# The first block of the down products in another order of groups, with seven pairs of tiles in seven products instead of five

## The chip, the cores and the metric

The kernel runs on one core of a Trainium2 chip. The metric is the time of one execution on the device, in microseconds (us). Five engines of the core work side by side, each through its own instructions in order: TensorE (PE in the profile), VectorE (DVE), ScalarE (ACT), GpSimd (POOL) and SyncE (SP), whose queue issues the transfers from memory.

## The reference

One decoder layer on 256 tokens of width 2048, in float32: a half feed-forward, retention and sliding-window attention side by side, a second half feed-forward, and a gated per-layer embedding. The change touches the feed-forward, which occurs twice (f1 and f2):

```python
D_MODEL, SEQ, D_FF = 2048, 256, 5632

def swiglu(x, w_gu, w_down):
    g, u = jnp.split(x @ w_gu, 2, axis=-1)
    return (jax.nn.silu(g) * u) @ w_down

h = layer_norm(alpha * h + 0.5 * swiglu(h, w_ffn1_gu[i], w_ffn1_down[i]), ln_g[i, 0], ln_b[i, 0])
...   # mixers
h = layer_norm(alpha * h + 0.5 * swiglu(h, w_ffn2_gu[i], w_ffn2_down[i]), ln_g[i, 2], ln_b[i, 2])
```

The down product `@ w_down` sums over 5632 = 44 tiles of 128 activations and gives 2048 columns.

## The kernel before, in words

**Numbers in two parts.** Every operand of a product is split into a high and a low part (`split`, L100 and L101): ScalarE casts the value to the high part (hi), VectorE subtracts to get the low part (lo). A product is three matmuls (`Sum.add`, L376 to L378): low by high, high by high, high by low. Each matmul here has 512 columns.

**Pairs and their two ways.** A pair p is two of the 44 tiles (p runs from 0 to 21). A block of the down product makes all 256 tokens of 1024 columns, which are two halves of tokens by two column blocks of 512. For one pair that is a 2 by 2 by 2 product of tiles. Done plainly ("P") it takes eight products, 24 matmuls; its weights are two chunks of 128x1024 (`Single`), for each of them one cast and one subtraction. Done in sevens ("S", class `Seven`) it takes seven products, 21 matmuls: the weights' two raw chunks are first combined by four VectorE additions of 128x512 (L172 to L175), then split in four pieces (VectorE instructions: `lf` 128x1024, `bf` 128x512, `luf` and `lvf` 128x1024), eight VectorE instructions in all, with four casts on ScalarE. The seven products of one S are in the order p1, q2, q3, q5, p7, p6, q4; the last S of a block has them in the order p1, q5, p6, p7, q2, q3, q4. After the last S of a block `fold` adds the sums that the sevens share (`seven_common`) to the residual.

**Activations.** The gu stage leaves the activations in 11 groups of four tiles, group g holding the pairs 2g and 2g+1. `convert(g)` splits a group in high and low part (f1ah, f1al). A group that is used in sevens needs `seven_forms` too: four VectorE additions of 128x256 (L447 to L450), a cast on ScalarE and a subtraction on VectorE (f1forms). `SEVEN_DOWN = (6, 7, 8, 9)` names the groups that have these sums; the second block (d1, columns 1024 to 2047) uses all eight of their pairs as S, in turn with P, and isn't touched by the change.

**Order.** Each engine's order is the program's. `down_units` lists the units of the first block (d0) and of the second (d1); `block` walks the list, calls `before_unit(u)` ahead of unit u, and takes each unit's weights from a queue. The queue is planned in the same order: after a unit is used, `fill` makes the next ones (cast, subtract, and the additions of an S) while the units that stand ready have less than 45 matmuls, and issues loads as long as slots are free. So VectorE gets its work for weights some 36 to 45 matmuls ahead of TensorE, in program order, and the work for activations is put between by `before_unit(u)`: it converts one group ahead of each even u, four units before the group is used, and makes the forms. VectorE's instructions do not wait for that point of the program on TensorE, only for their data and for a free slot. In f1 the rotary table (`rotary_table`, L820 to L850) is woven in during the first units of d0 as well.

**The first block before.** P0 to P11 (groups 0 to 5), then S12 P13 S14 P15 S16 P20 S17 P21 S18 P19: five S. The forms of groups 6 to 9 are made ahead of units 2, 4, 6 and 8, while the plain pairs run.

Of the kernel before, what the change touches and what calls it, by code (L numbers as in the profile page):

```python
# [15 lines left out]
P = 128  # L16
S = 256
# [9 lines left out]
KF = FF // P  # L27
# [18 lines left out]
AHEAD_SLOTS = 32  # L46

SEVEN_DOWN = (6, 7, 8, 9)

BIG = 3.0e38  # L50
MAGIC = 12582912.0
# [6 lines left out]
def layer(ctx: ExitStack, tc: tile.TileContext, io):  # L58
# [16 lines left out]
    def slot(shape, dt, name):  # L75
        return slots.tile(shape, dt, tag="slot", name=name)
# [22 lines left out]
    def split(dst_hi, dst_lo, src, lo_engine=None):  # L99
        act.copy(dst_hi, src)  # L100
        (lo_engine or dve).tensor_tensor(dst_lo, src, dst_hi, ALU.subtract)  # L101
# [200 lines left out]
    def slots_for_weights(n, ahead=45, far=90):  # L302
        room.update(slots=n, ahead=ahead, far=far)
# [136 lines left out]
    def seven_forms(full, hi, lo):  # L440


        a11, a21 = (full[:, 0::2, t * P : (t + 1) * P] for t in range(2))
        a12, a22 = (full[:, 1::2, t * P : (t + 1) * P] for t in range(2))
        raw = slot([P, 8, P], F32, "sums")
        f5, f6, f7, f3 = (raw[:, 2 * j : 2 * j + 2, :] for j in range(4))
        dve.tensor_tensor(f5, a21, a22, ALU.subtract)  # L447
        dve.tensor_tensor(f7, a11, a21, ALU.subtract)
        dve.tensor_tensor(f6, f5, a11, ALU.subtract)
        dve.tensor_tensor(f3, a12, f6, ALU.add)  # L450
        split(hi, lo, raw)
        return lambda e: [(hi[:, 2 * j + e, :], lo[:, 2 * j + e, :]) for j in range(4)]
# [295 lines left out]
    def load_columns(src, col, name):  # L748
        v = slot([P, 2, 512], F32, f"{name}{col}")
        sync.dma_start(v, src[col])  # L750
        return v
# [64 lines left out]
    def rotary_table(nm):  # L816

        inv, sgn = (0, 2) if nm == "r" else (1, 3)
        pos_i = slot([P, S], I32, "pos_i" + nm)
        act.dma_start(pos_i, io["positions"].broadcast_to([P, S]))  # L820
        pos = slot([P, S], F32, "pos" + nm)
        yield
        dve.tensor_copy(pos, pos_i)
        table = slot([P, 2, S], F32, "trig" + nm)
        cos, sin = trig[nm] = table[:, 0, :], table[:, 1, :]
        w = slot([P, 4, S], F32, "rot" + nm)
        ang, n, na, nb = (w[:, j, :] for j in range(4))
        dve.tensor_scalar(ang, pos, cst[:, inv : inv + 1], None, ALU.mult)
        dve.tensor_scalar(n, ang, INV_2PI, MAGIC, ALU.mult, ALU.add)
        dve.tensor_scalar(n, n, MAGIC, None, ALU.subtract)  # L830
        dve.tensor_scalar(na, n, 1.0 / 2048.0, MAGIC, ALU.mult, ALU.add)
        dve.tensor_scalar(na, na, MAGIC, 2048.0, ALU.subtract, ALU.mult)
        dve.tensor_tensor(nb, n, na, ALU.subtract)
        yield
        for who, j in ((na, 0), (nb, 0), (na, 1), (nb, 1), (na, 2), (nb, 2), (na, 3)):
            dve.scalar_tensor_tensor(ang, who, -TWO_PI[j], ang, ALU.mult, ALU.add)
            if who is nb:
                yield
        yield
        dve.tensor_scalar(n, ang, 3.1415925, -3.1415925, ALU.min, ALU.max)  # L840
        yield
        act.activation(nb, n, AF.Sin)
        yield
        dve.tensor_scalar(sin, nb, cst[:, sgn : sgn + 1], None, ALU.mult)
        dve.tensor_scalar(na, ang, 1.5707963267948966, None, ALU.add)
        dve.tensor_scalar(n, na, 3.141592653589793, -6.283185307179586, ALU.is_gt, ALU.mult)
        dve.tensor_tensor(na, na, n, ALU.add)
        dve.tensor_scalar(na, na, 3.1415925, -3.1415925, ALU.min, ALU.max)
        yield
        act.activation(cos, na, AF.Sin)  # L850
        yield
# [13 lines left out]
    def down_units(n_held):  # L865


        first = [("P", p) for p in range(2 * SEVEN_DOWN[0])]
        g = SEVEN_DOWN[0]
        sevens = [2 * h for h in SEVEN_DOWN[:3]] + [2 * SEVEN_DOWN[2] + 1, 2 * SEVEN_DOWN[3]]  # L870
        plain = [p for p in range(2 * g, KF // 2) if p not in sevens]
        plain = [p for p in plain if p < 2 * SEVEN_DOWN[2]] + sorted(
            (p for p in plain if p >= 2 * SEVEN_DOWN[2]), key=lambda p: p < 2 * SEVEN_DOWN[3] + 2
        )
        while sevens or plain:
            for kind, of in (("S", sevens), ("P", plain)):
                if of:
                    first.append((kind, of.pop(0)))
        plain = [p for p in range(KF // 2) if p // 2 not in SEVEN_DOWN]
        second = [("P", p) for p in plain[:2]]  # L880
        rest = plain[2:]
        for g in SEVEN_DOWN:
            for e in range(2):
                second += [("S", 2 * g + e), ("P", rest.pop(0))]
        return first, second + [("P", p) for p in rest[:-n_held]], rest[-n_held:]
# [4 lines left out]
    def plan_ffn(name):  # L890
        for j in range(KF // 4):
            block_units(gu_units(name, j), gu_keys(name, j))
        first, second, held = down_units(HELD_PAIRS[name == "f2"])
        block_units(first, down_keys(name, 0))
        block_units(second, down_keys(name, 1))
        plan.extend(Single(down_keys(name, 1)(n, p)) for n in range(2) for p in held)

    def ffn(name, i, ht, norm, keep, residual, keepers, away):
# [3 lines left out]
        raws = []  # L902
        made = {}
# [18 lines left out]
        def convert(g):  # L922
            hi, lo = (slot([P, 4, S], F32R, f"{name}a{w}{g}") for w in "hl")
            split(hi, lo, raws[g])
            acts[g] = hi, lo

        for j in range(KF // 4):
# [40 lines left out]
            if got:  # L968
                g, v = got
# [14 lines left out]
        def others(n, ahead=45):  # L984

            slots_for_weights(SLOTS - 4 - n - (2 if lazy else 0), ahead, max(90, ahead + 12))
# [3 lines left out]
        space = big.tile([P, 2 * len(SEVEN_DOWN), 8, P], F32R, tag="ht", name=name + "forms")  # L990
        made = {}
        first, second, held = down_units(HELD_PAIRS[name == "f2"])
        n_of = {}
        for b, units in enumerate((first, second + [("P", p) for p in held])):
# [10 lines left out]
        def before_unit(u):  # L1005
            if u == 0 and name == "f1":
                lazy.append(rotary_table("r"))
            g = u // 2 + 2
            others(2 * KF // 4 - max(0, KF // 4 - 1 - g) + (2 if u >= 10 else 0))
            if u % 2 == 0:  # L1010
                if 2 <= u < 2 + 2 * len(SEVEN_DOWN):
                    at = u // 2 - 1
                    made[SEVEN_DOWN[at]] = seven_forms(raws[SEVEN_DOWN[at]], space[:, 2 * at], space[:, 2 * at + 1])
                if g < KF // 4:
                    convert(g)
            if u in (11, 12):
                y[u - 11] = load_columns(residual, u - 11, name + "y")

        pn = [banks(f"{name}d{n}") for n in range(2)]
        sums = [[Sum(pn[n][t], n_of[0][t, n]) for n in range(2)] for t in range(2)]  # L1020
        block(f"{name}d0", first, down_keys(name, 0), lhs, forms, sums, fold(0), before_unit)
        for n in range(2):
            for t in range(2):
# [20 lines left out]
        pt_ = [banks(f"{name}e{t}") for t in range(2)]  # L1044
        sums = [[Sum(pt_[t][n], n_of[1][t, n]) for n in range(2)] for t in range(2)]
        block(f"{name}d1", second, down_keys(name, 1), lhs, forms, sums, fold(1), before_unit)
        slots_for_weights(27, last_ahead, last_ahead + 24)
        steps = [(down_keys(name, 1)(n, p), 2 * p, n) for n in range(2) for p in held]
# [747 lines left out]
```

## Time and profile before

| | |
|---|---|
| Time, median of 3 runs | 2273.39 us (2273.1 to 2273.79) |
| The profiled execution's own time | 2273.49 us |
| Its span in the profile | 2271.6 us |
| Busy in the span | PE 2264.0, DVE 1988.7, ACT 1221.7 us |
| First block d0 of f1 (first f1d to first f1e matmul) | 470.26 to 587.44 us |
| First block d0 of f2 | 1937.52 to 2054.69 us |

In the profile's rows a start and a duration in us stand first, then the engine, the line of the kernel, the operation, and output <- input by the program's names, with buffer numbers left out. `x2` behind a row means that so many neighbours are merged, and brackets at the end tell how long the engine had been idle before and what ended that. A matmul's duration overlaps with the next one's, so its pace is read from the distance of starts. In a table by stretches, each engine has its busy time and in brackets its count of instructions, followed by the granted TensorE clock (1.00 is full), the busy share of the DMA engines and the GB/s.

### The profile page before, as it was taken

Reading aid. Unit: us, or ns where it says so; the run is one execution under the profiler, and the core shown is the slowest. Engines: PE = TensorE matmul, PEld = TensorE weight load, DVE = VectorE, ACT = ScalarE, POOL = GpSimd, SP = SyncE. Lnnn points to the kernel's source line nnn. Section 1 sums busy time; section 2 is a strip of 40 time slices with the busy share of each in tenths; the row PEclk is TensorE's granted clock in tenths of the full one; section 3 lists DMA queues with packets and bytes.
Section 4 is the critical chain, followed back from the end, with each engine's and each line's share of the span. In section 5 each row is a group of like instructions: output and inputs, shape, how many; then the busy total and the mean of one; then the engine's idle time right before and its main releaser. Section 6 shows DMA issues by size and latency. Waiting matters only on the chain.

```text
span 2271.6 us, 29114 instructions
## 1 busy us (share of the span) xinstructions
PE 2264.0 (100%) x10503; PEld 1880.7 (83%) x10503; DVE 1988.7 (88%) x2574; ACT 1221.7 (54%) x1489; POOL 2.3 (0%) x9
## 2 busy tenths in 40 slices
PE   9999999999999999999999999999999999999999
PEld 8888888888888888888778888888888888888887
DVE  7999999999988887787789787789999999889887
ACT  6555555556555444544566454555555565555543
POOL 0000000000000000000000000000000000000000
PEclk9999999999999999999999999999999999999999
DMA  8666665665677789655456567887767766656872
GB/s 301 204 203 196 197 211 178 205 204 189 211 290 257 259 306 309 222 163 168 143 156 220 190 206 270 298 287 231 269 210 251 258 199 215 198 185 215 288 271 74
DMA packets 207736, 505.75 MB, mean 223 GB/s; under 512 B 16092, under 2 KB 20060, under 8 KB 207592
## 3 DMA queue, kind: packets, MB, share of 16 engines
q1 hardware_dynamic: 205608, 501.32, 65.6%
q10 hardware_dynamic: 1984, 2.58, 0.4%
q8 instruction: 82, 1.34, 0.2%
q14 instruction: 62, 0.51, 0.1%
HBM read 478.67 MB, written 25.17 MB: 222 GB/s over the span
## 4 chain that ended last, share of the span: by engine, by line
PE 98%; DVE 1%; DMA 0%; issue 0%; ACT 0%; ACTq 0%; POOL 0%; DVEq 0%; POOLq 0%
PE f1g L378 3%; PE f1g L376 3%; PE f1g L377 3%; PE f2g L378 3%; PE f2g L376 3%; PE f2g L377 3%; PE rqk L327 3%; PE f1u L376 2%; PE f1u L378 2%; PE f1u L377 2%; PE f2u L376 2%; PE f2u L378 2%; PE f2u L377 2%; PE aqk L327 2%; PE f1d L378 2%; PE f1d L377 2%
## 5 line engine op out<-in xcount | busy, mean ns | idle before, releaser
L101 DVE TENSOR_TENSOR lf_gu<-rf_gu,hf_gu 128x1024 fp32r<-128x1024 f32 (+1 forms) x276 | 325.5, 1212 | 14.1 <-ACT hf_gu L100 13.2
L100 ACT CAST hf_gu<-rf_gu 128x1024 fp32r<-128x1024 f32 (+1 forms) x276 | 275.5, 1043 | 29.6 <-DMA rf_gu<-in_f_gu 28.6
L101 DVE TENSOR_TENSOR lw_in_f<-rw_in_f,hw_in_f 128x1024 fp32r<-128x1024 f32 x140 | 167.3, 1219 | 34.4 <-ACT hw_in_f L100 34.4
L101 DVE TENSOR_TENSOR lf_down<-rf_down,hf_down 128x1024 fp32r<-128x1024 f32 x150 | 178.8, 1220 | 16.7 <-ACT hf_down L100 15.2
L100 ACT CAST hf_down<-rf_down 128x1024 fp32r<-128x1024 f32 x150 | 151.9, 1050 | 48.8 <-DMA rf_down<-in_f_down 21.7
L100 ACT CAST huf_gu<-uf_gu 128x1024 fp32r<-128x1024 f32 x70 | 73.8, 1054 | 146.5 <-DVE uf_gu L173 140.6
L100 ACT CAST hw_in_f<-rw_in_f 128x1024 fp32r<-128x1024 f32 x140 | 140.0, 1050 | 1.9 <-PE ga0b L377 0.6
L378 PE MATMUL f1g<-lf_gu,xt 128*128 128x512 f32 x247 | 96.4, 390 | 0.0
L376 PE MATMUL f1g<-hf_gu,xt 128*128 128x512 f32 x247 | 96.3, 390 | 0.0
L377 PE MATMUL f1g<-hf_gu,xt 128*128 128x512 f32 x247 | 96.1, 389 | 0.0
L100 ACT CAST hvf_gu<-vf_gu 128x1024 fp32r<-128x1024 f32 x70 | 73.8, 1055 | 29.7 <-DVE vf_gu L175 28.8
L973 ACT ACTIVATE eve<-eve 128x1024 f32<-128x1024 f32 x20 | 21.2, 1061 | 125.6 <-DVE eve L972 125.6
L376 PE MATMUL f2g<-hf_gu,ht 128*128 128x512 f32 x223 | 87.0, 390 | 0.0
L378 PE MATMUL f2g<-lf_gu,ht 128*128 128x512 f32 x223 | 86.9, 390 | 0.0
L377 PE MATMUL f2g<-hf_gu,ht 128*128 128x512 f32 x223 | 86.8, 389 | 0.0
L101 DVE TENSOR_TENSOR luf_gu<-uf_gu,huf_gu 128x1024 fp32r<-128x1024 f32 x70 | 85.3, 1219 | 0.0
L101 DVE TENSOR_TENSOR lvf_gu<-vf_gu,hvf_gu 128x1024 fp32r<-128x1024 f32 x70 | 85.3, 1218 | 0.0
L376 PE MATMUL f1u<-hf_gu,xt 128*128 128x512 f32 x212 | 83.3, 393 | 0.0
L377 PE MATMUL f1u<-hf_gu,xt 128*128 128x512 f32 x212 | 82.5, 389 | 0.0
L378 PE MATMUL f1u<-lf_gu,xt 128*128 128x512 f32 x212 | 82.5, 389 | 0.0
L376 PE MATMUL f2u<-hf_gu,ht 128*128 128x512 f32 x180 | 71.3, 396 | 0.0
L378 PE MATMUL f2u<-lf_gu,ht 128*128 128x512 f32 x180 | 70.1, 389 | 0.0
(1441 smaller groups left out, 6531.1 us busy)
## 6 DMA issues: line engine op xcount, KB each, us to landing
rf_gu<-in_f_gu SPq DMA_DIRECT2D x358, 512.0 KB
rf_down<-in_f_down SPq DMA_DIRECT2D x176, 512.0 KB
rw_in_f<-in_w_in_f SPq DMA_DIRECT2D x148, 512.0 KB
rw_rv<-in_w_rv SPq DMA_DIRECT2D x32, 512.0 KB
rw_ret<-in_w_ret SPq DMA_DIRECT2D x32, 512.0 KB
rw_mix<-in_w_mix SPq DMA_DIRECT2D x32, 512.0 KB
rw_pg<-in_w_pg SPq DMA_DIRECT2D x32, 512.0 KB
rw_att<-in_w_att SPq DMA_DIRECT2D x16, 512.0 KB
```

What stands on the lines that cost most here:

```text
L100: act.copy(dst_hi, src)
L101: (lo_engine or dve).tensor_tensor(dst_lo, src, dst_hi, ALU.subtract)
L327: pe.matmul(ps[f], hi[:, kk, f * P : (f + 1) * P], rhs(k), start=k == 0, stop=k == n_k - 1,)
L376: pe.matmul(o, al, bh, start=first, stop=False)
L377: pe.matmul(o, ah, bh, start=False, stop=False)
L378: pe.matmul(o, ah, bl, start=False, stop=self.left == 0)
L973: act.activation(g, g, AF.Silu)
```

## The change

The first block now takes the groups in the order `DOWN_ORDER = (0, 1, 6, 2, 7, 3, 8, 4, 9, 5, 10)`, both pairs of a group one after the other. The pairs of groups 6 to 9 are S up to pair 18, so that seven pairs (12 to 18) are in sevens. The units are P0 P1 P2 P3 S12 S13 P4 P5 S14 S15 P6 P7 S16 S17 P8 P9 S18 P19 P10 P11 P20 P21. `before_unit` makes the forms of a group in the same place as its conversion: of group 6 ahead of unit 0, 7 ahead of unit 4, 8 ahead of unit 8, 9 ahead of unit 12. The number of forms and conversions is the same. The second block's list is the same.

```diff
+DOWN_ORDER = (0, 1, 6, 2, 7, 3, 8, 4, 9, 5, 10)
...
     def down_units(n_held):
-        first = [("P", p) for p in range(2 * SEVEN_DOWN[0])]
-        g = SEVEN_DOWN[0]
-        sevens = [2 * h for h in SEVEN_DOWN[:3]] + [2 * SEVEN_DOWN[2] + 1, 2 * SEVEN_DOWN[3]]
-        plain = [p for p in range(2 * g, KF // 2) if p not in sevens]
-        plain = [p for p in plain if p < 2 * SEVEN_DOWN[2]] + sorted(
-            (p for p in plain if p >= 2 * SEVEN_DOWN[2]), key=lambda p: p < 2 * SEVEN_DOWN[3] + 2
-        )
-        while sevens or plain:
-            for kind, of in (("S", sevens), ("P", plain)):
-                if of:
-                    first.append((kind, of.pop(0)))
+        first = [("S" if g in SEVEN_DOWN and 2 * g + e < 2 * SEVEN_DOWN[-1] + 1 else "P", 2 * g + e) for g in DOWN_ORDER for e in range(2)]
...
         def before_unit(u):
             if u == 0 and name == "f1":
                 lazy.append(rotary_table("r"))
-            g = u // 2 + 2
-            others(2 * KF // 4 - max(0, KF // 4 - 1 - g) + (2 if u >= 10 else 0))
-            if u % 2 == 0:
-                if 2 <= u < 2 + 2 * len(SEVEN_DOWN):
-                    at = u // 2 - 1
-                    made[SEVEN_DOWN[at]] = seven_forms(raws[SEVEN_DOWN[at]], space[:, 2 * at], space[:, 2 * at + 1])
-                if g < KF // 4:
-                    convert(g)
+            n = u // 2 + 2
+            others(2 * KF // 4 - max(0, KF // 4 - 1 - n) + (2 if u >= 10 else 0))
+            if u % 2 == 0 and n < KF // 4:
+                g = DOWN_ORDER[n]
+                if g in SEVEN_DOWN:
+                    at = SEVEN_DOWN.index(g)
+                    made[g] = seven_forms(raws[g], space[:, 2 * at], space[:, 2 * at + 1])
+                convert(g)
```

## The prediction

> **What bounds the kernel now.** I read the page's totals first, then what TensorE (PE) waited for, then the two stretches that the change rewrites, then PE's and VectorE's (DVE's) instructions in them one by one.
>
> ```profile
> span 2271.6 us, 29114 instructions
> ...
> PE 2264.0 (100%) x10503; PEld 1880.7 (83%) x10503; DVE 1988.7 (88%) x2574; ACT 1221.7 (54%) x1489; POOL 2.3 (0%) x9
> ```
>
> ```profile
> PE warm L1675 <- POOL ident masks.py:199: 1.4, 1, 1.4
> ...
> PE lnps L625 <- DVE mixy L613: 0.2, 1, 0.2
> ```
>
> PE is busy for 2264.0 of 2271.6 us. Only five groups of waits on PE are named in the whole trace, the first of 1.4 us and the last of 0.2 us, none of them in a down product. So PE bounds the kernel, and a matmul less is worth its full pitch as long as PE goes on without waits.
>
> ```profile
> core 0: us, PE busy (x) PEld busy (x) DVE busy (x) ACT busy (x) POOL busy (x), PEclk, DMA share, GB/s
> 470.00:587.00 117.00, 117.00 (x522) 96.94 (x521) 107.95 (x135) 69.13 (x74) 0.00 (x0) 1.00 0.57 194
> 1937.00:2054.50 117.50, 117.50 (x525) 97.36 (x524) 103.08 (x116) 68.29 (x72) 0.00 (x0) 1.00 0.56 194
> ```
>
> ```profile
> rf_down<-in_f_down SPq DMA_DIRECT2D x176, 512.0 KB
> ```
>
> The two rows by stretch are the first down block (d0) of the first and of the second feed-forward. PE is busy all the time, the granted clock is 1.00. The column that matters is DVE's: 107.95 of 117.00 us and 103.08 of 117.50 us. DVE prepares every weight chunk, and here it has 9.0 and 14.4 us to spare, less than the page's 88% suggests. Whatever is added to DVE in d0 has to fit into that, and at the right moment.
>
> ```profile
> 470.26 0.39 PE L376 MATMUL f1d<-hf_down,f1al 128*128 128x512 f32 x1
> ...
> 478.19 0.40 PE L378 MATMUL f1d<-lf_down,f1ah 128*128 128x512 f32 x1
> 478.43 1.04 PE L916 MATMUL f1t<-ident,evw 128*128 128x128 f32 x8
> 479.22 0.48 PE L376 MATMUL f1d<-hf_down,f1al 128*128 128x512 f32 x1
> ...
> 536.44 0.39 PE L376 MATMUL f1d0s<-hf_down,f1al 128*128 128x512 f32 x1
> ...
> 587.44 0.39 PE L376 MATMUL f1e<-hf_down,f1al 128*128 128x512 f32 x1
> ...
> 2054.69 0.39 PE L376 MATMUL f2e<-hf_down,f2al 128*128 128x512 f32 x1
> ```
>
> Pitch: from the first row to the row at 478.19 there are 35 steps (a plain pair has 24 matmuls, a chunk 12; this is one pair and one chunk), so 7.93 / 35 = 0.2266 us per matmul. A plain pair (P) takes 24 x 0.2266 = 5.44 us, a pair in sevens (S) 21 x 0.2266 = 4.76 us. The eight transposes push the stream back by 0.8 us. The first d0 begins at 470.26 and ends at 587.44, where f1e begins; 513 x 0.2266 + 0.8 = 117.1 us against 117.2. The second ends at 2054.69. There is no wait in either.
>
> **What the change removes.** d0 had 17 P and 5 S; it gets 15 P and 7 S. That is 2 x 3 = 6 matmuls fewer per feed-forward, 12 in all: 12 x 0.2266 = 2.7 us off the bound engine, 0.12% of the kernel. No other PE work changes, and what follows d0 is the same. About 0.2%, 4.5 us, is what a measurement can tell from no change, so this gain alone would be no difference.
>
> **What it adds and moves.** The prices on DVE, as distances from one start to the next:
>
> ```profile
> 475.27 1.22 DVE L101 TENSOR_TENSOR f1al<-f1a,f1ah 128x1024 fp32r<-128x1024 f32 x1
> 476.41 2.35 DVE L101 TENSOR_TENSOR lf_down<-rf_down,hf_down 128x1024 fp32r<-128x1024 f32 x2
> 478.68 0.29 DVE L823 CAST posr<-pos_ir 128x256 f32<-128x256 int32 x1
> ...
> 484.91 0.42 DVE L447 TENSOR_TENSOR sums<-f1a 128x256 f32<-128x256 f32 x1
> ...
> 487.58 1.22 DVE L101 TENSOR_TENSOR f1forms<-sums,f1forms 128x1024 fp32r<-128x1024 f32 x1 [1.12 <-ACT f1forms L100]
> 488.72 1.22 DVE L101 TENSOR_TENSOR f1al<-f1a,f1ah 128x1024 fp32r<-128x1024 f32 x1
> ```
>
> ```profile
> 527.36 0.68 DVE L172 TENSOR_TENSOR uf_down<-rf_down,rf_down 128x512 f32<-128x512 f32 x1
> ...
> 531.22 0.69 DVE L101 TENSOR_TENSOR bf_down<-rf_down,bf_down 128x512 fp32r<-128x512 f32 x1
> ...
> 534.09 1.22 DVE L101 TENSOR_TENSOR lf_down<-rf_down,hf_down 128x1024 fp32r<-128x1024 f32 x1
> ```
>
> ```profile
> 475.20:505.00 29.80, 6.76 (x19) 0.84 (x2) 1.00 0.54 177
> ```
>
> A split of an activation group (C, f1al) takes 476.41 - 475.27 = 1.14 us. The two chunks of a P take 478.68 - 476.41 = 2.27 us. One set of sums of activations (F) takes 488.72 - 484.91 = 3.81 us, of which 1.12 us is a wait for ScalarE's cast. The eight instructions of an S take 534.09 - 527.36 = 6.73 us; its first part (b11 and b21, needed first) is there after 531.22 - 527.36 = 3.86 us. The rotary table, which the first feed-forward weaves in, is 6.76 us, with the 0.3 us cast before it 7.0 us.
>
> So an S costs DVE 6.73 us where PE spends 4.76 us on it, a P 2.27 us where PE spends 5.44. Two S for two P add 2 x (6.73 - 2.27) = 8.9 us to each d0. That would just about use up the 9.0 us of spare time in the first and fit into the 14.4 us of the second, if it were spread evenly. It isn't. The block now runs P0 P1 P2 P3 S12 S13 P4 P5 S14 S15 P6 P7 S16 S17 P8 P9 S18 P19 P10 P11 P20 P21. Each F comes four units ahead of its S S, together with the C of the same group. One round of four units, S S P P, costs PE 2 x 4.76 + 2 x 5.44 = 20.4 us, and DVE 2 x 6.73 + 2 x 2.27 + 3.81 + 2 x 1.14 = 24.1 us. DVE loses 3.7 us a round for as long as the rounds last, and all F and C of the block but one C lie before S18's weights. Only the last five units, all P, leave DVE idle, when that is of no use any more. Before, the twelve P came first and all F lay beside them.
>
> The lead with which DVE enters is small: four plain units, and in the first feed-forward the rotary table lies in them too. In the old order S12's last part was ready at about 534.1 while PE began S12 at 536.44 (row above): a lead of a few us after twelve plain units, which the new order does not have before its first S.
>
> Now the column, in the order in which the built kernel issues DVE's work. In both feed-forwards it starts where the last gu block's output is multiplied and the old order would do its next C (475.27, and 1942.54 below). Until the last part of S18 come 4 F, 8 C, the chunks of 8 P (P2 to P9) and 7 S:
>
> 4 x 3.81 + 8 x 1.14 + 8 x 2.27 + 7 x 6.73 = 15.24 + 9.12 + 18.16 + 47.11 = 89.6 us, in the first feed-forward 96.6 us with the table.
>
> ```profile
> 1942.54 1.22 DVE L101 TENSOR_TENSOR f2al<-f2a,f2ah 128x1024 fp32r<-128x1024 f32 x1
> ...
> 2012.23 1.23 DVE L101 TENSOR_TENSOR f2al<-f2a,f2ah 128x1024 fp32r<-128x1024 f32 x1 [1.38 <-ACT f2ah L100]
> ...
> 2035.74 0.69 DVE L172 TENSOR_TENSOR uf_down<-rf_down,rf_down 128x512 f32<-128x512 f32 x1 [1.44 <-DMA rf_down<-in_f_down]
> ```
>
> First: 475.27 + 96.6 = 571.9. Second, in the time of the old trace: 1942.54 + 89.6 = 2032.2. From there PE has 13 matmuls of S18 to go (it is the last S, with its v sums third and fourth of seven) and five P: 13 x 0.2266 + 5 x 5.44 = 30.1 us. The blocks end at 602.0 and 2062.3 instead of 587.44 and 2054.69: 14.6 and 7.6 us later, with the saved matmuls already in. Sum: 22.2 us.
>
> That DVE is really the later one all along, step by step in the first block: PE could begin S12 at 470.26 + 4 x 5.44 + 0.8 = 492.8. DVE has done F and C, P2, P3, the C of the group after, 4 of the 7 us of the table and the first part of S12 at 493.7: 0.5 us lost. S13's first part is ready at 501.7, PE wants it at 498.5: 3.2 us. P4's second chunk lies behind F and C and is ready at 511.9: 2.8 us. So it goes on: S14 0.7, S15 2.0, P6 2.6, S17 1.1, P8 2.6, S18 0.6; together 16 us, less 1.4 us of saved matmuls. In the second block, without the table, the first wait is at P4 (1.2), then S15 1.1, P6 2.6, S17 1.1, P8 2.6, S18 0.6: 9.1 us.
>
> Costed at nothing: the loads on SP's queue change order but not number; SP's waits for free slots sit a whole S or more ahead of use, as I count the units between issue and use. ScalarE has 69.13 us of PE's 117 in the first window and gains 2 casts of about 1 us for each further S, hidden beside DVE. The fold after S18 comes five units before the end instead of one, on a DVE that is then ahead. If one of these covers went, the cost is that of the loads rival below. What follows d0 finds DVE no later than before relative to PE (both wait for the end of d0 to add the residual), and as PE is full everywhere else, a delay of d0 is not won back.
>
> The two unknowns are how much DVE waits beyond the four 1.12 us. Below: if ScalarE's casts were hidden in all eight F, 8 x 1.12 = 9.0 us would go. Above: the first d0 had 9.0 - 4.5 = 4.5 us of other DVE waits, the second 14.4 - 4.5 = 9.9. The row at 2012.23 shows their kind: DVE behind ScalarE's cast into a slot that PE still held, with DVE far ahead. A DVE that is late doesn't meet that, so I take nothing, and as the end of the range the first block's 4.5 us in both, 9 us.
>
> The profiled execution took 2273.49 us (span 2271.6 and 1.9 around it), 0.1 above the median of 2273.39, so the sum stands against either: 2273.5 + 22.2 = 2295.7, say **2296 us**, +1.0%.
>
> **Rivals.** (A) DVE's lead covers the added work, PE keeps its pace: 2273.5 - 2.7 = 2270.8 us, no measurable change. For it: no wait of PE in any d0 before, 9.0 and 14.4 us of DVE time left against 8.9 needed. Against it: the table of units above, where the spare time comes after the last S. It decides if S13's first part is ready by 498.5. Chance 0.05. This is the case on the other side: not slower.
> (B) The loads of two S in a row come late. The row at 2035.74 shows DVE waiting 1.44 us for a raw chunk of an S. If each of the 14 S met that, 14 x 1.44 = 20 us more: 2316. Against it: a DMA share of 0.57 and 194 GB/s in the window, and a round of eight chunks of 512 KB (0.524 MB, row above) in 24.1 us needs 174. Chance 0.05.
> (C) PE's clock drops in the new waits of 2 to 3 us. No wait over 1.4 us is in the trace, so nothing here shows it. If the 24 matmuls after each of the seven waits of 2 us or more ran at half rate, 7 x 5.44 = 38 us at most, less where DVE is late anyway: up to 2334. Chance 0.04. [...]
>
> **Numbers.** Forecast 0.86, A 0.05, B 0.05, C 0.04. Faster by over 0.2% needs more than the saved matmuls give: 0.01, out of A's 0.05; within 0.2% the other 0.04 of A; slower 0.95. The range is the forecast with both unknowns: 2295.7 - 9 = 2287 to 2295.7 + 9 = 2305; it leaves out A, B and C.
>
> **What would show it.** In the profile after: PE idle in both d0 stretches and nowhere else new, about 16 and 9 us, released by DVE's splits of seconds of pairs (P4, P6, P8) and first parts of S13, S15, S17; DVE without gaps there but the 1.12 us before each f1forms; d0 about 132 and 125 us instead of 117; DVE idle in the five plain units at the end; clock 1.00. Wrong would be: PE without waits in d0 (A), waits that end on DMA (B), a granted clock under 1 (C), or most of the loss outside d0.

## The result, and the profile after

| | median of the runs | against the kernel before |
|---|---|---|
| before | 2273.59 us (2273.1 to 2274.49) | |
| changed | 2296.57 us (2295.78 to 2297.11) | 1.0101, 95% interval 1.0089 to 1.0113 |

The change makes the kernel 1.0% slower, 23.0 us. The page of the changed kernel begins so:

```profile
span 2294.5 us, 29133 instructions
...
PE 2268.5 (99%) x10491; PEld 1877.7 (82%) x10491; DVE 2005.8 (87%) x2598; ACT 1227.4 (53%) x1497; POOL 2.3 (0%) x9
```

There are 12 matmuls fewer, and still the span is 22.9 us longer. Both first blocks, from their first f1d or f2d matmul to the first matmul of the second block:

```profile
470.40:602.70 132.30, 120.63 (x517) 96.08 (x516) 119.61 (x151) 71.85 (x79) 0.00 (x0) 0.99 0.51 174
1952.40:2077.50 125.10, 118.50 (x516) 95.21 (x515) 113.00 (x131) 70.95 (x77) 0.00 (x0) 1.00 0.51 179
```

They last 132.3 and 125.1 us (117.2 each before): 15.1 and 7.9 us more, which together are the whole 23.0 us. In the first, PE is busy for 120.6 of 132.3 us, DVE for 119.6. The waits of PE in the two stretches (us in total, times, longest):

```profile
PE f1d0s L380 <- DVE lf_down L103: 5.7, 4, 2.9
PE f1d L378 <- ACT hf_down L102: 3.1, 3, 1.3
PE f1d L380 <- DVE lf_down L103: 2.7, 3, 0.9
```

```profile
PE f2d L380 <- DVE lf_down L103: 2.7, 3, 0.9
PE f2d L378 <- ACT hf_down L102: 2.2, 2, 1.1
PE f2d0s L380 <- DVE lf_down L103: 1.5, 2, 0.8
```

There was none of these before. Nearly all are for a low part from VectorE (L103 is the subtraction) or for a high part from ScalarE (L102), whose queue stands behind the forms' cast just as VectorE's does. In TensorE's own rows, the first weights of S13, the second chunk of P4 and the ends of the two blocks (first row of f1e and of f2e):

```profile
502.02 0.50 PE L380 MATMUL f1d0s<-lf_down,f1ah 128*128 128x512 f32 x1 [2.94 <-DVE lf_down L103]
...
510.68 0.50 PE L378 MATMUL f1d<-hf_down,f1al 128*128 128x512 f32 x1 [1.31 <-ACT hf_down L102]
...
602.66 0.39 PE L378 MATMUL f1e<-hf_down,f1al 128*128 128x512 f32 x1
...
2077.51 0.39 PE L378 MATMUL f2e<-hf_down,f2al 128*128 128x512 f32 x1
```

VectorE in the first block: its first instruction of the new order and the last part of S18's weights; then what it waited for in between:

```profile
475.39 0.42 DVE L449 TENSOR_TENSOR sums<-f1a 128x256 f32<-128x256 f32 x1
...
571.09 1.22 DVE L103 TENSOR_TENSOR lvf_down<-vf_down,hvf_down 128x1024 fp32r<-128x1024 f32 x1
```

```profile
DVE f1forms L103 <- ACT f1forms L102: 4.5, 4, 1.2
DVE vf_down L176 <- DVE uf_down L175: 0.5, 1, 0.5
```

So VectorE worked from 475.39 to 572.3 without a gap, but for the four waits for the forms' cast and one of 0.5 us. It is the engine that sets the end of the block.

### The profile page after: what moved, and what is told of

Read it like the earlier page. It is cut to its first block, busy times and chain, and to the rows that moved or that the text cites. A ratio compares the mean times of both kernels' runs of the same rounds, so it can differ in the third digit from the quotient of the medians.

```text
span 2294.5 us, 29133 instructions
## 1 busy us (share of the span) xinstructions
PE 2268.5 (99%) x10491; PEld 1877.7 (82%) x10491; DVE 2005.8 (87%) x2598; ACT 1227.4 (53%) x1497; POOL 2.3 (0%) x9
## 4 chain that ended last, share of the span: by engine, by line
PE 92%; DVE 5%; ACT 1%; issue 1%; DMA 1%; ACTq 0%; DVEq 0%
PE f1g L380 3%; PE f1g L378 3%; PE f1g L379 3%; PE f2g L380 3%; PE f2g L378 3%; PE f2g L379 3%; PE rqk L329 3%; PE f1u L380 2%; PE f1u L378 2%; PE f1u L379 2%; PE f2u L378 2%; PE f2u L380 2%; PE f2u L379 2%; PE aqk L329 2%; PE f2e L378 1%; PE f2e L379 1%
## 5 line engine op out<-in xcount | busy, mean ns | idle before, releaser
L103 DVE TENSOR_TENSOR lf_gu<-rf_gu,hf_gu 128x1024 fp32r<-128x1024 f32 (+1 forms) x276 | 325.4, 1211 | 13.7 <-ACT hf_gu L102 12.7
L102 ACT CAST hf_gu<-rf_gu 128x1024 fp32r<-128x1024 f32 (+1 forms) x276 | 275.5, 1043 | 31.5 <-DMA rf_gu<-in_f_gu 30.1
L103 DVE TENSOR_TENSOR lw_in_f<-rw_in_f,hw_in_f 128x1024 fp32r<-128x1024 f32 x140 | 167.3, 1219 | 34.5 <-ACT hw_in_f L102 34.5
L103 DVE TENSOR_TENSOR lf_down<-rf_down,hf_down 128x1024 fp32r<-128x1024 f32 x146 | 174.1, 1220 | 19.2 <-ACT hf_down L102 16.4
L102 ACT CAST hf_down<-rf_down 128x1024 fp32r<-128x1024 f32 x146 | 149.1, 1050 | 60.2 <-DMA rf_down<-in_f_down 22.2
L102 ACT CAST huf_gu<-uf_gu 128x1024 fp32r<-128x1024 f32 x70 | 73.8, 1054 | 146.2 <-DVE uf_gu L175 140.3
L102 ACT CAST hw_in_f<-rw_in_f 128x1024 fp32r<-128x1024 f32 x140 | 139.9, 1050 | 2.4 <-DMA rw_in_f<-in_w_in_f 1.8
L102 ACT CAST hvf_gu<-vf_gu 128x1024 fp32r<-128x1024 f32 x70 | 73.8, 1054 | 29.4 <-DVE vf_gu L177 28.5
L103 DVE TENSOR_TENSOR luf_gu<-uf_gu,huf_gu 128x1024 fp32r<-128x1024 f32 x70 | 85.3, 1219 | 0.0
L103 DVE TENSOR_TENSOR lvf_gu<-vf_gu,hvf_gu 128x1024 fp32r<-128x1024 f32 x70 | 85.3, 1218 | 0.0
```

## The experiments

A ratio is to the kernel before, which ran beside each kernel on the same chip (medians 2273.4 to 2273.6 us). A difference to the changed kernel is one of medians of separate runs. "Column" is the summed work of VectorE up to the last S's weights. The code excerpts are shortened: `units("...")` stands for the list comprehension that makes the list of units from such a string.

**Five S in the changed order.** Is it the order or the two more S?

```diff
-        first = [("S" if g in SEVEN_DOWN and ... else "P", 2 * g + e) for g in DOWN_ORDER for e in range(2)]
+        first = units("P0 P1 P2 P3 S12 S13 P4 P5 S14 S15 P6 P7 S16 P17 P8 P9 P18 P19 P10 P11 P20 P21")
```

> The changed order with five pairs in sevens instead of seven (S17 and S18 are plain again), so TensorE's work is that of before. The theory (VectorE's summed work up to the last S's weights sets the end of the first block): 3 F, 6 C, 6 P, 5 S and the table come before S16's weights, 9 plain units follow; worked out in the same way as the prediction, the first block ends 12.1 us late in f1 and 5.0 us late in f2, 2273.6 + 17.1 = 2291 us. The rival (the two more S, 8.9 us of VectorE work a block, are the cause): without them VectorE's total is that of before, so no loss, 2273.6 us.

Measured: 2294.43 us, ratio 1.0094 (1.0077 to 1.011). The rival's 2273.6 is out: with before's number of S and of matmuls the new order alone costs 21 us. The theory's 2291 is 3.4 us too low. One omission is plain in VectorE's and TensorE's rows behind S16, now the last S:

```profile
557.57 0.68 DVE L484 TENSOR_TENSOR evw<-eve,f1d0s 128x512 f32<-128x512 f32 x1
...
562.48 2.35 DVE L103 TENSOR_TENSOR lf_down<-rf_down,hf_down 128x1024 fp32r<-128x1024 f32 x2
...
563.76 0.50 PE L380 MATMUL f1d<-lf_down,f1ah 128*128 128x512 f32 x1 [0.95 <-DVE lf_down L103]
```

The fold (here its first and the first row behind it, from 557.57 to 562.48, 4.9 us) now stands ahead of P9's chunks, while VectorE is still behind, and TensorE waits another 0.95 us there. I had left it out of the column. It explains about 2 us of the 3.4 in the two blocks; the rest was not traced.

**S and P strictly in turn.** Is it that two S stand together?

```diff
+        first = units("P0 P1 P2 P3 S12 P4 S13 P5 S14 P6 S15 P7 S16 P8 S17 P9 S18 P19 P10 P11 P20 P21")
```

> The same seven S and the same 15 P as in the changed kernel, but S and P strictly in turn from S12 on (S12 P4 S13 P5 S14 P6 S15 P7 S16 P8 S17 P9 S18, then the five plain units). The theory: the work of VectorE ahead of S18's weights is the same to the instruction, so the blocks end as late as in the changed kernel, 2296 to 2297 us, with the waits spread in other places. The rival (two S in a row are the cause: 13.5 us of VectorE work against 9.5 us of TensorE's): an S and a P together take VectorE 9.0 us and TensorE 10.2, so most waits go, and what remains is F and C beyond that: 2280 us or less.

Measured: 2296.45 us, ratio 1.0101 (1.0086 to 1.0116), the changed kernel's time to 0.1 us. TensorE's waits lie elsewhere, fewer and longer:

```profile
PE f1d0s L380 <- DVE lf_down L103: 8.1, 4, 3.6
PE f2d0s L380 <- DVE lf_down L103: 6.7, 2, 3.4
```

So how the S are spaced between the fourth unit and S18 doesn't matter; what VectorE has to do before the last of them does.

**The forms' cast with work beside it.** The same instructions, ordered so that VectorE splits the group while ScalarE casts the forms.

```diff
-        made[g] = seven_forms(raws[g], ...); convert(g)
+        act.copy(hi_of_group, raws[g])       # first
+        # four additions; act.copy(hi, raw)  # the forms' cast
+        dve.tensor_tensor(lo_of_group, raws[g], hi_of_group, ALU.subtract)
+        dve.tensor_tensor(lo, raw, hi, ALU.subtract)
```

> The changed kernel with another order of the same instructions where a group's forms are made: the cast of the group's conversion is issued first, and its subtraction stands between the cast and the subtraction of the forms, so that VectorE works during the 1.12 us in which it waits for ScalarE's cast. The theory: four times about 1.1 us less of VectorE's column in each block, all ahead of S18: 2 x 4.4 = 8.8 us less, 2296.6 - 8.8 = 2288 us. The rival (the price is one per wait of TensorE, for restarting, and not VectorE's time): the number of waits stays about the same, so 2295 to 2297 us.

Measured: 2287.11 us, ratio 1.006 (1.0045 to 1.0075), 9.5 us less than the changed kernel. TensorE still waits four times for parts of S in the first block (total, times, longest), as in the changed kernel (5.7, 4, 2.9, above), so the price isn't one per wait:

```profile
PE f1d0s L380 <- DVE lf_down L103: 5.2, 4, 2.5
```

**More VectorE work early, and late.** The same four extra subtractions (128x1024, 4.6 us a block) at two places of the changed kernel: the same subtraction repeated.

```diff
+            if u == 6:      # the other run: u == 17, with group 10
+                for _ in range(4):
+                    dve.tensor_tensor(lo_of_group_3, raws[3], hi_of_group_3, ALU.subtract)
```

> The changed kernel with one subtraction of the activations' split (group 3, 128x1024) done five times instead of once ahead of unit 6, that is 4 x 1.14 = 4.6 us more of VectorE's work in each first block, ahead of S14. The theory: every us ahead of the last S's weights comes out as a us of time, 2 x 4.55 = 9.1 us, 2296.6 + 9.1 = 2305.7 us. The rival (VectorE still has spare time that takes part of it, 12.5 us of the changed block's 132 in which it is not busy): clearly less than that, 2297 to 2301 us.

Measured early: 2306.23 us, ratio 1.0146 (1.013 to 1.0161), 9.7 us more than the changed kernel for 9.1 us of added work as worked out. Such four extra subtractions take 5.0 us in the rows of the run with the late ones (582.60, below); by that it is some 10 us in the two blocks, so the work ahead of the last S costs its own time: one to one within 0.5 us.

> The changed kernel with the same four extra subtractions per first block as in the run with more VectorE work early, but ahead of unit 17 (group 10), behind the weights of the last S. The theory: VectorE is ahead of TensorE there and sits idle at the end of the block, so 4.6 us more cost nothing: 2296 to 2297 us. The rival (all VectorE work of the block counts, wherever it stands): 2306 us as with the early ones.

Measured late: 2301.95 us, ratio 1.0126 (1.011 to 1.0141), 5.4 us more; between the two. VectorE's and TensorE's rows say why:

```profile
581.47 1.22 DVE L994 SCALAR_TENSOR_TENSOR f1y<-f1y,evw 128x1024 f32<-128x1024 f32 x1
582.60 5.00 DVE L1011 TENSOR_TENSOR f1al<-f1a,f1ah 128x1024 fp32r<-128x1024 f32 x4
587.52 3.49 DVE L103 TENSOR_TENSOR lf_down<-rf_down,hf_down 128x1024 fp32r<-128x1024 f32 x3
...
588.79 0.50 PE L380 MATMUL f1d<-lf_down,f1ah 128*128 128x512 f32 x1 [2.06 <-DVE lf_down L103]
```

Ahead of unit 17 VectorE is ahead, but it has just done the fold, and its lead on P11 is smaller than the 4.9 us that the four instructions took: TensorE waits 2.1 us for P11's first chunk, and the block lasts 134.6 instead of 132.3 us (the second 127.4 instead of 125.1). Half of the work was free and half was not, so both the theory and the rival are off. I had taken the idle time at the end of the block as there from S18 on; it comes only after the fold and the next chunks.

**The rotary table behind the last S.**

```diff
-            if u == 0 and name == "f1":
+            if u == 17 and name == "f1":
                 lazy.append(rotary_table("r"))
```

> The changed kernel with the rotary table of the first feed-forward started ahead of unit 17 instead of unit 0, so that its 7.0 us of VectorE work stand behind the last S's weights. The theory: 6.9 us off the first block of f1, nothing in f2: 2289.7 us, and the first block of f1 loses then about as much as that of f2 (7 to 8 us). The rival (f1 loses more than f2 for another reason, such as transfers): 2296 us.

Measured: 2289.14 us, ratio 1.0069 (1.0055 to 1.0083), 7.4 us less than the changed kernel for 7.0 us of table. The first block of f1 then lasts 125.1 us (470.27 to 595.33), as long as f2's (125.1). So the table is all of the difference between the two.

**The groups' low parts on GpSimd.**

```diff
-            split(hi, lo, raws[g])
+            split(hi, lo, raws[g], pool)
```

> The changed kernel with the low part of each activation group (C's subtraction, 11 in each feed-forward) computed on GpSimd instead of VectorE. The theory: 8 x 1.14 = 9.1 us less in VectorE's column ahead of S18 in each block; f1 keeps about 6 us of loss, f2 none: 2278 to 2280 us, provided that GpSimd does not slow VectorE down and is done in time. The rival (the two disturb each other): VectorE's instructions of 1.22 us take longer while GpSimd runs, and part of the gain or all of it is lost: 2285 to 2296 us.

Measured: 2314.59 us, ratio 1.0182 (1.0168 to 1.0196), 18 us worse than the changed kernel, and beyond the 2285 to 2296 us of the rival too. One such subtraction on GpSimd and the one that VectorE ran meanwhile:

```profile
511.96 2.48 POOL L103 TENSOR_TENSOR f1al<-f1a,f1ah 128x1024 fp32r<-128x1024 f32 x1 [24.77 <-ACT f1ah L102]
...
512.87 2.65 DVE L103 TENSOR_TENSOR lf_down<-rf_down,hf_down 128x1024 fp32r<-128x1024 f32 x1 [0.68 <-ACT hf_down L102]
```

VectorE's instruction, 1.22 us for all 39 of its kind in the changed kernel's first block, took 2.65 us: it ends 1.1 us after GpSimd's does (511.96 + 2.48 = 514.44, and 515.52), as if it had begun only then. The next pair reads alike: GpSimd's is done at 518.57 + 3.06 = 521.63, and an addition of VectorE (L174), 0.68 us in the changed kernel, starts at 519.29, takes 2.89 us and ends 0.55 us later. What holds VectorE in these rows was not traced. GpSimd takes 2.40 to 3.35 us for what VectorE does in 1.22 (nine subtractions each, between 470 and 600 us). VectorE lost more than it was relieved of: there the nine took it 11.0 us in the changed kernel, and now 36 subtractions of weights take 1.56 us in the mean instead of 1.22, 12.2 us more, and the seven additions of L174 1.00 instead of 0.68, 2.2 us more. The first block lasts 140.1 us against 132.3 in the changed kernel.

**A version against both.** The kernel before, with seven S late, the forms made beside plain pairs as before, and the cast with work beside it (the diff shows only the order). First with P20 behind S16:

```diff
-        first = [("P", p) for p in range(2 * SEVEN_DOWN[0])]
...
+        first = units("P0 P1 P2 P3 P4 P5 P6 P7 P8 P9 S12 P10 S13 S14 P11 S15 S16 P20 S17 P21 S18 P19")
```

> A version against both: the kernel before with seven S in its first block, in the order P0 to P9, S12 P10 S13 S14 P11 S15 S16 P20 S17 P21 S18 P19, the forms made beside plain pairs as before, and VectorE's wait for the cast in each F filled with the group's conversion (1.1 us less per F). The theory: the plain pairs first build the lead that the S later use up; worked out unit by unit no wait remains, so only the 12 saved matmuls show: 2273.4 - 2.7 = 2270.7 us. The rival (seven S are too many for VectorE in any order): 8.9 us of added work against 4.4 us won back a block, so waits remain, 2274 to 2279 us.

Measured: 2272.56 us, ratio 0.9996 (0.9988 to 1.0005). One new wait was left, for the low part of group 10, which is converted one unit before P20 uses it:

```profile
PE f1d L376 <- DVE f1al L101: 1.7, 1, 1.7
```

Then with P19, P20, P21 in the places of P20, P21, P19:

> The version before it with one thing mended: there, the only new wait was 1.7 us at P20, whose group 10 is converted just one unit ahead of its use. Now P19 (group 9, converted three units ahead) stands there, and P20 and P21 come one plain unit later: P0 to P9, S12 P10 S13 S14 P11 S15 S16 P19 S17 P20 S18 P21. The theory: no wait is left in either first block, both end 1.36 us sooner than before: 2273.4 - 2.7 = 2270.7 us. The rival (seven S need more than VectorE has in the first block of f1, with the table in it): a wait of about 2 us stays there, 2272.5 us as before the mending.

Measured: 2271.66 us (2271.01 to 2272.33, before 2273.01 to 2274.37), ratio 0.9991 (0.9982 to 1.0). The first and last rows of its two first blocks:

```profile
470.27 0.39 PE L376 MATMUL f1d<-hf_down,f1al 128*128 128x512 f32 x1
...
586.34 0.39 PE L376 MATMUL f1e<-hf_down,f1al 128*128 128x512 f32 x1
...
1937.60 0.39 PE L376 MATMUL f2d<-hf_down,f2al 128*128 128x512 f32 x1
...
2053.41 0.39 PE L376 MATMUL f2e<-hf_down,f2al 128*128 128x512 f32 x1
```

116.1 and 115.8 us, against 117.2: 1.1 and 1.4 us less, where the six saved matmuls of a block are worth 1.36, and no wait of TensorE is named in either. So the theory's mechanism holds, but the time, 1.9 us less than before where 2.7 were expected, lies between the theory's and the rival's; one wait of 0.3 us at the first S of the second down block (columns 1024 to 2047) of f1 is part of what is missing. The interval ends at 1.0, so this is a small gain at the edge of what can be told, though no run of the one overlaps with one of the other.

And the same order with the cast waited for:

> The same order as in the mended version, but with the forms' cast waited for as in the kernel before (1.12 us in each F). It tells how much of that version is the order and how much the filled waits. The theory: in f1 VectorE's lead is used up at S14 (0.7 us) and S16 (2.9 us), the block ends 2.4 us late; f2 has the lead of 7 us more that the table does not take there, no wait, 1.4 us sooner: 2273.4 + 1.0 = 2274.4 us. The rival (only the number of S in the block counts, 8.9 us of added work): both blocks lose, 2280 us or more.

Measured: 2276.92 us, ratio 1.0014 (1.0005 to 1.0023). The rival is out, since f2 has no wait and gains; the theory's 2274.4 is 2.5 us too low. f1 waits twice:

```profile
PE f1d0s L378 <- DVE lf_down L101: 4.0, 2, 2.7
```

These are S14 (1.4) and S16 (2.7), where 0.7 and 2.9 were worked out. f2's block gains its 1.35 us (1941.52 to 2057.34), f1's loses 3.4 where 2.4 were worked out. That is 2.1 us in the two blocks; the profiled execution, 2276.02 us, was 0.9 faster than the median, and where the others lost more was not traced. So the late order alone does not gain: it needs the waits for the cast filled as well.

## Why the prediction came out

2296 us was forecast, 2296.57 measured, and by the mechanism that was named: VectorE's column up to the last S sets the end of each block. The single waits came out less exactly than their sum.

- *The column.* VectorE was to have S18's last part ready at 571.9; it was at 571.09 + 1.22 = 572.3. The blocks were to end at 602.0 and 7.6 us late; they end at 602.66 and last 125.1 instead of 117.2, 7.9 us more.
- *The waits.* The time in brackets counts from the end of the matmul before, which overlaps with the next one, so it leaves out about 0.16 us of each wait. I take distances of starts, less the pitch of 0.23 us. S13 3.2 forecast, 3.1 in the trace; P4 2.8, there 1.5 for the high and 1.1 for the low part of the same chunk; S12, S14, S15 0.5, 0.7, 2.0, there 0.6, 0.9, 1.8. With 15 x 24 + 7 x 21 = 507 matmuls the first block lost 132.3 - (507 x 0.2266 + 0.8) = 16.6 us where the prediction's waits add up to 16, the second 9.4 where they add up to 9.1. I had put the waits of P4, P6 and P8 down to VectorE alone. In the first block about half of each is ScalarE's cast, which in its own queue stands behind the forms' cast, and that waits for VectorE's additions; ScalarE's rows ahead of P4's second chunk:

```profile
507.68 1.05 ACT L102 CAST f1forms<-sums 128x1024 fp32r<-128x1024 f32 x1 [2.19 <-DVE sums L452]
508.64 1.04 ACT L102 CAST f1ah<-f1a 128x1024 fp32r<-128x1024 f32 x1
509.58 2.94 ACT L102 CAST hf_down<-rf_down 128x1024 fp32r<-128x1024 f32 x3
```

- *Where I was wrong in the small.* "Clock 1.00" did not hold all the time. After P6's two waits the clock dropped once in f1:

```profile
536.63 0.50 PE L378 MATMUL f1d<-hf_down,f1al 128*128 128x512 f32 x1 [1.13 <-ACT hf_down L102]
536.97 0.40 PE L379 MATMUL f1d<-hf_down,f1ah 128*128 128x512 f32 x1
538.27 0.80 PE L380 MATMUL f1d<-lf_down,f1ah 128*128 128x512 f32 x1 [0.91 <-DVE lf_down L103]
538.86 0.63 PE L378 MATMUL f1d<-hf_down,f1al 128*128 128x512 f32 x1
...
541.42 0.41 PE L378 MATMUL f1d<-hf_down,f1al 128*128 128x512 f32 x1
```

```profile
538.00:540.00 2.00, 1.73 (x4) 1.45 (x5) 2.00 (x3) 2.00 (x3) 0.00 (x0) 0.50 0.99 358
```

The seven matmuls from 538.86 to 541.42 came 0.43 us apart instead of 0.2266. That is rival C's mechanism, at about 1.4 us of TensorE's time. C's sum put 24 matmuls at half rate behind each of seven waits; no rows of the runs show so many: the longest stretches in them have 12, as in the run with S and P in turn from 535.76 to 541.04, after a wait of 3.4 us, and the one here has seven. It cost next to nothing: VectorE set the pace, TensorE came to S17 later, and the wait of 1.1 us forecast there is missing from the trace. That the clock stayed up after S13 was luck: in four of the other runs it dropped there (last section), which the prediction, with 0.04 for C, took for unlikely.
- *The unknowns.* VectorE's waits beyond the forms' cast came to 0.5 us in the first block's column and none in the second's, near the nothing that was taken, and far from the 4.5 us at the end of the range. The run with the cast hidden shows what the low end was worth: 9.5 us.
- *A sign that did not come.* VectorE was to be idle in the five plain units at the end. In the first block it works on from S18's last part to 590.9 us without a gap, on the next chunks and the fold, and is idle only in the 12 us behind that.
- *What it rested on.* The runs show the order as the cause (five S: +21 us), the spacing as no cause (in turn: the same time), and VectorE's work ahead of the last S as worth one to one (9.7 for some 10, -7.4 for -7.0, -9.5 for -9.0: waits of 4.5 in each of the two blocks).
- *Rival A* needed S13's first part by 498.5; TensorE waited 2.9 us for it. *Rival B*: none of PE's waits in d0 ends on a DMA.

## What to carry to other kernels

Before work is moved from a full engine to one that is 88% busy, add up the second engine's work in its own order up to the last point at which the first needs it, and compare with the first one's clock; shares over a whole kernel, or even over the stage, do not tell it, since the work ahead of that point cannot use the idle time behind it. Put cheap-to-feed work first and the work that draws on the lead last: the same seven S cost 23.0 us early, 3.4 late, and gained 1.9 late with the waits for the cast filled. A wait of the feeding engine for another's cast is worth filling with work that is there anyway.

## What the runs showed of the hardware that was not expected

The clock dropped after shorter waits than the 2 us or more of rival C, and not always after the same wait. In the changed kernel P6's two waits of 1.1 and 0.9 us with two matmuls between them were followed by half pace (rows above), while P4's two, of 1.3 and 0.9 us with the same between them, were followed by full pace:

```profile
510.68 0.50 PE L378 MATMUL f1d<-hf_down,f1al 128*128 128x512 f32 x1 [1.31 <-ACT hf_down L102]
511.01 0.40 PE L379 MATMUL f1d<-hf_down,f1ah 128*128 128x512 f32 x1
512.32 0.50 PE L380 MATMUL f1d<-lf_down,f1ah 128*128 128x512 f32 x1 [0.91 <-DVE lf_down L103]
512.65 0.40 PE L378 MATMUL f1d<-hf_down,f1al 128*128 128x512 f32 x1
512.89 0.39 PE L379 MATMUL f1d<-hf_down,f1ah 128*128 128x512 f32 x1
```

The single wait of 2.9 us at S13 was followed by full pace too. In four other runs (five S, the extra work early and late, GpSimd), whose units up to there are the same, S13's wait of 2.9 us was followed by half pace. So in the run with five S:

```profile
501.91 0.79 PE L380 MATMUL f1d0s<-lf_down,f1ah 128*128 128x512 f32 x1 [2.92 <-DVE lf_down L103]
502.49 0.63 PE L378 MATMUL f1d<-hf_down,f1al 128*128 128x512 f32 x1
502.92 0.63 PE L379 MATMUL f1d<-hf_down,f1ah 128*128 128x512 f32 x1
```

In the run with more work early, after a wait of 5.4 us:

```profile
520.86 0.39 PE L379 MATMUL f1d0s<-hf_down,f1ah 128*128 128x512 f32 x1
526.66 0.80 PE L380 MATMUL f1d0s<-lf_down,f1ah 128*128 128x512 f32 x1 [5.41 <-DVE lf_down L103]
```

```profile
526.00:530.00 4.00, 3.33 (x9) 2.66 (x10) 4.00 (x5) 2.08 (x3) 0.00 (x0) 0.57 0.00 0
530.00:534.00 4.00, 3.70 (x17) 2.76 (x16) 3.93 (x7) 2.83 (x3) 0.00 (x0) 1.00 0.74 259
```

The clock was 0.57 of full speed in the mean over the first 4 us and 1.00 over the next 4.

In the run with the low parts on GpSimd the same two waits of one chunk came out both ways: 1.13 and 1.94 us (540.68 and 543.35) were followed by full pace, 1.10 and 1.94 us (566.79 and 569.47) by half pace, six matmuls about 0.43 us apart. So the length of the waits alone does not tell which pace follows. What else decides it was not shown.
